# Second half of position 30's down weights as sixteen transfers of eight partitions

## The chip, the core and the metric

The kernel runs on one core of one Trainium2 chip. The metric is the device time of one execution in microseconds (us). Three runs of the kernel before took 1213.39 us (median), 1213.33 and 1214.49 us.

## The reference

One decoder layer over 256 tokens of width 1024, all in float32. The first part (a gated spatial MLP and a block attention, merged and normalised) ends near 270 us of the span and the change does not touch it. The second part is a routed feed-forward: each token goes to 4 of 32 experts, and for each expert

```
gu  = xe @ w_up[e] + b_up[e]          # w_up[e]: 1024 x 2048, 8 MB
g   = min(gu[:, :F], 7);  u = clip(gu[:, F:], -7, 7)
act = (u + 1) * (g * sigmoid(1.702 * g))
y   = act @ w_down[e] + b_down[e]     # w_down[e]: 1024 x 1024, 4 MB
```

The weighted sum of the experts' outputs is added to the residual and a last LayerNorm gives the result. Every expert's 12 MB of weights is read once, some 400 MB in all, for a few rows of tokens each.

## The kernel before

The 32 experts are sorted at run time into 32 positions; position 30 is the last but one. Each position has three steps: "a" and "b", the two halves of the up product, and "d", the down product. Each step's weights are two halves of 2 MB (128 partitions by 16 KB), named a0, a1, b0, b1, d0, d1. Positions 5 to 29 (`WHOLE`) load both halves of a step by one transfer of 4 MB; positions 30 and 31 load each half by its own.

The weights go into a ring of five buffers `R`, each of two half slots. `load_next(slot)` (line 176 and on) takes the next half in the list `order` and issues its transfer from the SyncE queue (SP), to the slot that was just released by the product that read it. So the order of transfers is that of the steps, and SP waits before a transfer for the product that frees the slot. Line 211 is the ordinary transfer. The last half of all (d1 of position 31) is cut by columns into four transfers of 512 KB, so that the last product can begin with the first quarter (line 209). The list ends:

```
... b0,b1 of 30   a0,a1 of 31   b0,b1 of 31   d0,d1 of 30   d0,d1 of 31
```

TensorE's order around these steps is written out: `step` calls `up_part` for a and b and `down_half` (line 729) for d, and between them small pieces that were put off by `later` (transposes of the activation, line 719; the spread of the routing weights, line 684; the scatter of a finished position, line 744). The down product of position 30 takes d0, then d1; then come the transposes for position 31 and the scatter of position 30, then d0 and the four quarters of d1 of position 31, and the last scatter. After that VectorE takes the statistics of the last LayerNorm (line 1124), a loop for left-over tokens is entered (line 1147), and four stores write the output.

Of the kernel before, what the change touches and what calls it, by code (L numbers as in the profile page):

```python
# [17 lines left out]
P = 128  # L18
# [6 lines left out]
NE = 32  # L25
# [2 lines left out]
WHOLE = range(5, 30)  # L28
LEFT_AT, RESIDUAL_AT, NORM_AT = 5, (7, 12), 17
W0, W1, W2, W3, W4, W5 = 9, 3, 9, 7, 5, 3  # L30
MS = {mybir.EngineType.PE}
STARTS = {mybir.EngineType.PE, mybir.EngineType.DVE, mybir.EngineType.Activation}

# [21 lines left out]
def tile_kernel(ctx: ExitStack, tc: tile.TileContext, x, ln_in_g, ln_in_b, w_in, gmlp_ln_g, gmlp_ln_b,  # L55
                w_spatial, b_spatial, w_branch_a, w_branch_b, w_out, ln_mix_g, ln_mix_b, w_router,
                b_router, w_up, b_up, w_down, b_down, ln_ffn_g, ln_ffn_b, out):
    nc = tc.nc
# [7 lines left out]
    def ps_mm():  # L66
        return bank["pool"].tile([P, 512], FT, name="mm", bufs=bank["mm"])
# [103 lines left out]
    def half(slot):  # L171
        return R[slot // 2][:, slot % 2 * 4096:slot % 2 * 4096 + 4096]
# [3 lines left out]
    def load_next(slot):  # L176
        done.append(slot)
        if len(ring) == len(order):
            return
        p, k = order[len(ring)]  # L180
        n = 2 if p in WHOLE else 1
        if len(done) < n:
            return
        slots = done[-n:]
        done.clear()
        for i, to in enumerate(slots):
            ring[p, k[0] + str(int(k[1]) + i)] = to
        if p not in expert_at:
            expert_at[p] = nc.values_load(dyn["ids"][0:1, p:p + 1], engines=[mybir.EngineType.SP], min_val=0,
                                          max_val=NE - 1)  # L190
        e, h = expert_at[p], int(k[1])
        if n == 2:
            assert h == 0 and slots[0] % 2 == 0 and slots[1] == slots[0] + 1
            to = R[slots[0] // 2]
        else:
            to = half(slot)
        if k[0] == "d":
            src = wd[e] if isinstance(e, int) else wd[bass.ds(e, 1)].rearrange("o p h n -> (o p) h n")
            if n == 2:
                to = to.rearrange("p (h n) -> p h n", h=2)  # L200
            else:
                src = src[:, h]
        else:
            src = wu[e] if isinstance(e, int) else wu[bass.ds(e, 1)].rearrange("o p n -> (o p) n")
            lo = 8192 * (k[0] == "b") + 4096 * h
            src = src[:, lo:lo + 4096 * n]
        if len(ring) == len(order):
            for j in range(4):
                nc.sync.dma_start(to[:, j * 1024:(j + 1) * 1024], src[:, j * 1024:(j + 1) * 1024])
        else:  # L210
            nc.sync.dma_start(to, src)

# [352 lines left out]
    for i in range(n_pieces):  # L565
# [29 lines left out]
        if nm == "A" and hf == 1:  # L595
            attend()
            for slot in (4, 5, 6, 7):
                load_next(slot)
        if nm == "B":
            to_T(G1, hTh, hTl, (hf,))  # L600
        if i >= n_pieces - 3:
            for slot in ((2, 3), (0,), (1,))[i - n_pieces + 3]:
                load_next(slot)
# [30 lines left out]
    sp2 = ctx.enter_context(tc.tile_pool(name="s2", bufs=1, reuse_waits="tile"))  # L634
    R.append(sp2.tile([P, 8192], FT, name="R4"))
    load_next(8)
    load_next(9)
    hT2 = sp2.tile([P, NC, 2 * GRP * CAP], FT, name="hT2")
# [438 lines left out]

    with tc.manual_schedule(engines=MS):
        def free(p, k):
            load_next(ring[p, k])  # L1080
# [66 lines left out]
    with tc.For_i(0, n_left) as i:  # L1147
# [27 lines left out]
        for j in range(2):  # L1175
            to = [ps_mm(), ps_mm()]
# [51 lines left out]
```

## Time and profile before

| | |
|---|---|
| median of three runs | 1213.39 us |
| the profiled execution's own time | 1214.27 us |
| its span, first to last instruction | 1212.6 us |
| mean granted TensorE clock | 0.964 |
| TensorE matmul busy | 1108.5 us (91%) |
| VectorE, ScalarE, GpSimd busy | 414.5, 214.9, 110.0 us |
| HBM read | 448.58 MB, 371 GB/s over the span |

The page gives the busy time of each engine, the span in 40 slices (from 333 us to 1182 us every slice has the DMA engines at 90% or more and 426 to 433 GB/s), the costliest groups of instructions with what ended the idle time before them, and the DMA transfers by line. The trace behind it answers for any stretch: an engine's instructions in order of time, who waited for whom, how long a transfer took from its issue to its landing (the moment its completion has fully arrived), and the mean busy share of the 16 DMA engines. Times are us from the span's start.

### The profile page before, as it was taken

What the parts mean: (1) busy time and instruction counts of PE and PEld (TensorE: products, weight loads), DVE (VectorE), ACT (ScalarE), POOL (GpSimd) and SP (SyncE); (2) the same over time, 40 slices, a digit from 0 to 9 for tenths busy, and PEclk for the clock granted to TensorE, in tenths of its full rate; (3) what the DMA queues carried; (4) which work ended last, traced back from release to release, by engine and by line L of the source; (5) the groups of instructions that cost most, each with busy time, mean ns of one, the idle gap of its engine ahead of it and who ended that gap; (6) DMA issues with size and microseconds to landing.
All of it is one profiled execution on the core that took longest, in us unless ns stands there. A gap on an engine that the chain in (4) does not pass through costs nothing. (4 is left out here: it accounts for less than half of the span.)

```text
span 1212.6 us, 21803 instructions
## 1 busy us (share of the span) xinstructions
PE 1108.5 (91%) x9725; PEld 578.8 (48%) x9725; DVE 414.5 (34%) x787; ACT 214.9 (18%) x355; POOL 110.0 (9%) x121
## 2 busy tenths in 40 slices
PE   8999999998989889889999998999999899999793
PEld 6777888874424343343444343434333434344231
DVE  7964645564323121313122231413222221221213
ACT  5445643422101000010000010101010100010010
POOL 2800200000000000001000000100100010100000
PEclk9999999999999989889999998999999998999888
DMA  9554557665899999999999999999999999999993
GB/s 355 188 208 147 222 186 303 252 255 236 337 429 433 430 430 430 431 431 431 430 432 430 430 433 430 431 429 430 430 433 432 431 430 430 431 431 430 426 428 135
DMA packets 44208, 451.06 MB, mean 372 GB/s; under 512 B 2968, under 2 KB 3628, under 8 KB 26064
## 3 DMA queue, kind: packets, MB, share of 16 engines
q1 hardware_dynamic: 43504, 449.47, 88.5%
q8 instruction: 78, 1.28, 0.4%
q10 hardware_dynamic: 608, 0.16, 0.1%
q14 instruction: 18, 0.15, 0.0%
HBM read 448.58 MB, written 1.05 MB: 371 GB/s over the span
## 5 line engine op out<-in xcount | busy, mean ns | idle before, releaser
L702 PE MATMUL mm<-R,hT 128*32 128x512 f32 x3136 | 378.4, 609 | 13.7 <-DMA R<-in_w_up_dram 13.7
L729 PE MATMUL at<-R,actT 128*32 128x256 f32 x3328 | 217.6, 402 | 17.6 <-DMA R<-in_w_down_dram 7.4
L702 PEld LDWEIGHTS mm<-R,hT 128*32 128x32 f32 x3136 | 89.8, 111 | 198.0 <-issue 173.9
L708 DVE TENSOR_SCALAR gg<-mm 64x512 f32<-64x512 f32 x49 | 33.5, 683 | 389.2 <-PE mm L702 389.2
L729 PEld LDWEIGHTS at<-R,actT 128*32 128x32 f32 x3328 | 100.7, 115 | 110.2 <-issue 29.9
L711 POOL TENSOR_TENSOR gg<-gg,sg 64x512 f32<-64x512 f32 x52 | 66.5, 1278 | 845.1 <-ACT sg L709 845.1
L479 DVE TENSOR_TENSOR wlo<-R,whi 128x1024 fp32r<-128x1024 f32 x80 | 112.4, 1416 | 76.1 <-ACT whi L471 75.7
L529 PE MATMUL mm<-whi,hTh 128*128 128x512 f32 x256 | 100.9, 402 | 0.8 <-ACT R L488 0.8
L529 PE MATMUL mm<-wlo,hTh 128*128 128x512 f32 x256 | 99.9, 398 | 0.5 <-DVE wlo L479 0.5
L529 PE MATMUL mm<-whi,hTl 128*128 128x512 f32 x256 | 99.9, 398 | 0.0
L471 ACT ACTIVATE whi<-R 128x1024 fp32r<-128x1024 f32 x80 | 84.3, 1056 | 86.7 <-PE mm L529 81.5
L709 ACT ACTIVATE sg<-gg 64x512 f32<-64x512 f32 x52 | 32.8, 631 | 284.9 <-DVE gg L708 261.4
L736 ACT ACTIVATE y<-at 128x256 f32<-128x256 f32 x52 | 20.0, 384 | 338.1 <-PE at L729 338.1
L661 PEld LDWEIGHTS tp<-pt,xn 128*128 128x128 f32 x464 | 58.6, 198 | 32.9 <-DVE hT L666 21.2
L661 PE MATMUL tp<-pt,xn 128*128 128x128 f32 (+2 forms) x464 | 69.0, 294 | 0.5 <-DVE pt L653 0.4
L744 PE MATMUL ac<-y,qt 32*128 32x256 f32 x832 | 60.6, 406 | 0.5 <-ACT y L736 0.5
L669 ACT ACTIVATE hT<-tp,lm 128x128 f32<-128x128 f32 (+2 forms) x58 | 25.8, 445 | 195.3 <-PE tp L661 195.3
L744 PEld LDWEIGHTS ac<-y,qt 32*128 32x128 f32 x832 | 38.1, 187 | 37.5 <-issue 35.2
L719 PEld LDWEIGHTS tp<-ident,act 64*128 64x128 f32 x208 | 28.8, 209 | 54.2 <-issue 17.2
L529 PEld LDWEIGHTS mm<-wlo,hTh 128*128 128x128 f32 x256 | 48.0, 188 | 12.9 <-DVE wlo L479 1.7
L721 DVE COPY actT<-tp 128x256 f32<-128x256 f32 x52 | 22.1, 425 | 93.7 <-PE tp L719 93.6
L529 PEld LDWEIGHTS mm<-whi,hTh 128*128 128x128 f32 x256 | 48.4, 190 | 11.8 <-ACT R L488 0.9
(265 smaller groups left out, 835.7 us busy)
## 6 DMA issues: line engine op xcount, KB each, us to landing
R<-in_w_up_dram SPq DMA_DIRECT2D x50, 4096.0 KB, 32.1
R<-in_w_down_dram SPq DMA_DIRECT2D x25, 4096.0 KB, 34.1
R<-in_w_up_dram SPq DMA_DIRECT2D x28, 2048.0 KB, 11.6
R<-in_w_in_dram SPq DMA_DIRECT2D x13, 2048.0 KB, 9.6
R<-in_w_down_dram SPq DMA_DIRECT2D x13, 2048.0 KB, 32.7
R<-in_w_branch_a_dram SPq DMA_DIRECT2D x2, 2048.0 KB
R<-in_w_branch_b_dram SPq DMA_DIRECT2D x2, 2048.0 KB, 9.0
R<-in_w_out_dram SPq DMA_DIRECT2D x2, 2048.0 KB
```

The source lines that it names most:

```text
L471: nc.scalar.activation(hi, w, AF.Copy)
L479: nc.vector.tensor_tensor(lo, w, hi.bitcast(FT), op=OP.subtract)
L529: nc.tensor.matmul(ps[t], (a_l if k == 1 else a_h)[:, c, t * P:(t + 1) * P], (lo if k == 2 else hi)[:, cc], start=c == 0 and k == 0, stop= ...
L661: nc.tensor.matmul(ps[:, i * w:(i + 1) * w], zn[:, t, c * P:(c + 1) * P], pt[:, t, :w], start=t == 0, stop=t == T - 1)
L669: nc.scalar.activation(dst[:, c, :w], ps[:, i * w:(i + 1) * w], AF.Identity, scale=lm[:, 0, c:c + 1], bias=lm[:, 1, c:c + 1])
L702: nc.tensor.matmul(ps[n * CAP:(n + 1) * CAP], xs[:, c], w[:, o:o + 512], start=False, stop=c == NC - 1)
L708: nc.vector.tensor_scalar(gg, ps[:2 * CAP], LIMIT, None, op0=OP.min)
L709: nc.scalar.activation(sg, gg, AF.Sigmoid, scale=SW_ALPHA)
L711: nc.gpsimd.tensor_tensor(gg, gg, sg, op=OP.mult)
L719: nc.tensor.transpose(ps[:, c * 2 * CAP:(c + 1) * 2 * CAP], v[:, c], ident[:2 * CAP, :2 * CAP])
L729: nc.tensor.matmul(py[n * CAP:(n + 1) * CAP, :256], at[:, c, h], w[:, o:o + 256], start=h == 0 and c == 0, stop=h == 1 and c == 3)
L744: nc.tensor.matmul(to[n // 2][:, n % 2, t * 256:(t + 1) * 256], qt[s, t], y[s], start=start and t == 0, stop=stop and t == T - 1)
```

## The change

`load_next` gets a third case. For d1 of position 30 the one transfer of 128 partitions by 16 KB becomes sixteen, each of eight partitions (128 KB). All other transfers, and every product, stay as they are.

```
+EIGHTHS = (NE - 2, "d1")
 ...
         if len(ring) == len(order):
             for j in range(4):
                 nc.sync.dma_start(to[:, j * 1024:(j + 1) * 1024], src[:, j * 1024:(j + 1) * 1024])
+        elif (p, k) == EIGHTHS:
+            for j in range(0, P, 8):
+                nc.sync.dma_start(to[j:j + 8], src[j:j + 8])
         else:
             nc.sync.dma_start(to, src)
```

## Rows read from the trace of the kernel before

**Rows 1.** Costliest groups: instruction, count | busy us, mean ns | idle before, releaser.
```profile
L729 PE MATMUL at<-R,actT 128*32 128x256 f32 x3328 | 217.6, 402 | 17.6 <-DMA R<-in_w_down_dram 7.4
```

**Rows 2.** Timeline of PE at the end: start us, us, instructions, [idle before <-releaser].
```profile
1180.63 1.93 PE L729 MATMUL at<-R,actT 128*32 128x256 f32 x32 [0.16 <-SPq L1147]
1185.50 1.93 PE L729 MATMUL at<-R,actT 128*32 128x256 f32 x32 [2.94 <-SPq L1147]
...
1188.94 1.15 PE L744 MATMUL ac<-y,qt 32*128 32x256 f32 x16
1190.37 2.37 PE L729 MATMUL at<-R,actT 128*32 128x256 f32 x40 [0.28 <-DMA R<-in_w_down_dram]
...
1195.40 0.64 PE L729 MATMUL at<-R,actT 128*32 128x256 f32 x8 [0.61 <-DMA R<-in_w_down_dram]
```

**Rows 3.** DMA issues at 1114.05, 1140.69, 1146.69, 1154.33: KB, us to landing.
```profile
R<-in_w_up_dram SPq DMA_DIRECT2D x1, 2048.0 KB, 37.4
R<-in_w_down_dram SPq DMA_DIRECT2D x1, 2048.0 KB, 39.9
R<-in_w_down_dram SPq DMA_DIRECT2D x1, 2048.0 KB, 38.8
R<-in_w_down_dram SPq DMA_DIRECT2D x1, 2048.0 KB, 36.0
```

**Rows 4.** Stretches: us, busy of PE, PEld, DVE, ACT, POOL, PEclk, DMA share, GB/s.
```profile
1182.60:1185.50 2.90, 0.00 (x0) 0.00 (x0) 0.68 (x1) 0.00 (x0) 0.68 (x1) 1.00 0.86 362
1185.50:1187.40 1.90, 1.90 (x33) 0.97 (x33) 0.00 (x0) 0.00 (x0) 0.00 (x0) 1.00 0.52 222
```

**Rows 5.** DMA in 1186 to 1198: packets in all, and queue 8's share.
```profile
DMA packets 341, 1.73 MB, mean 144 GB/s; under 512 B 41, under 2 KB 41, under 8 KB 300
...
q8 instruction: 1, 0.02, 0.6%
```

**Rows 6.** Timeline of SP, transfers as issued: start us, us, line, count.
```profile
1114.05 24.45 SPq L211 DMA_DIRECT2D R<-in_w_up_dram  x6
1140.69 0.33 SPq L211 DMA_DIRECT2D R<-in_w_down_dram  x1
1146.69 0.33 SPq L211 DMA_DIRECT2D R<-in_w_down_dram  x1
...
1156.39 0.33 SPq L209 DMA_DIRECT2D R<-in_w_down_dram  x1
...
1170.91 0.33 SPq L209 DMA_DIRECT2D R<-in_w_down_dram  x1
```

**Rows 7.** Waits of SP's queue, 1138 to 1172: us in total, times, longest.
```profile
SPq L209 <- DMA R<-in_w_up_dram: 14.1, 4, 4.3
```

**Rows 8.** DMA in 0 to 3.3: all packets, and ScalarE's queue (q10).
```profile
DMA packets 90, 0.31 MB, mean 93 GB/s; under 512 B 8, under 2 KB 16, under 8 KB 90
...
q10 hardware_dynamic: 16, 0.00, 0.5%
```

**Rows 9.** Issue cost on SP: line 209's duration in ns; five issues without a wait.
```profile
L209 SPq DMA_DIRECT2D R<-in_w_down_dram x4: 333/333/337, 1156.4 to 1170.9; - x4
...
17.12 0.40 SPq L219 DMA_DIRECT2D R<-in_gmlp_ln_g_dram  x1
...
19.48 0.60 SPq L223 DMA_DIRECT2D R<-in_b_up_dram  x1
```

**Rows 10.** Transfers into an empty queue (268 to 269.2, and the stores).
```profile
R<-in_w_up_dram SPq DMA_DIRECT2D x2, 2048.0 KB, 7.2
...
out_dram<-R SPq DMA_DIRECT2D x4, 256.0 KB, 2.0
```

**Rows 11.** An earlier wait: PE timeline, then two stretches as in rows 4.
```profile
1127.16 3.64 PE L702 MATMUL mm<-R,hT 128*32 128x512 f32 x16 [5.02 <-DMA R<-in_w_up_dram]
...
1125.90:1129.30 3.40, 2.14 (x12) 0.59 (x16) 0.00 (x0) 0.00 (x0) 0.00 (x0) 0.50 1.01 434
1129.30:1132.70 3.40, 3.40 (x24) 1.22 (x16) 0.00 (x0) 0.00 (x0) 0.00 (x0) 0.50 0.98 419
```

More of the change, by code (lines that the diff above doesn't have):

```diff
@@ L30 @@
 W0, W1, W2, W3, W4, W5 = 9, 3, 9, 7, 5, 3
+EIGHTHS = (NE - 2, "d1")
 MS = {mybir.EngineType.PE}
@@ L209, in load_next @@
                 nc.sync.dma_start(to[:, j * 1024:(j + 1) * 1024], src[:, j * 1024:(j + 1) * 1024])
+        elif (p, k) == EIGHTHS:
+            for j in range(0, P, 8):
+                nc.sync.dma_start(to[j:j + 8], src[j:j + 8])
         else:
```

## Prediction, made before the changed kernel ran

> **What bounds the kernel now.** I read the page's busy times and 40 slices first (TensorE 91% busy, DMA engines full from 333 us on), then the costliest groups, then the last 30 us by timeline. A busy TensorE does not settle what bounds the end: the down product's idle time is ended by weights [rows 1], and at the end every product of a down half starts when its weights land. Adding the time to landing to the issue times, d0 of position 30 lands at 1140.69 + 39.9 = 1180.59, d1 at 1146.69 + 38.8 = 1185.49, d0 of position 31 at 1154.33 + 36.0 = 1190.33 [rows 3]; the products start at 1180.63, 1185.50 and, with the first quarter, 1190.37, and the last quarter's at 1195.40 [rows 2]. So the last landing sets the end: 1195.4, then 0.64 us of matmuls to 1196.04 and an unchanged tail of 16.6 us to 1212.6.
>
> Two more things are to be seen there. First, the 16 DMA engines do not run level. After 1186 only 1.73 MB are moved [rows 5], yet d0 and d1 of position 31 (4.19 MB) have still to land: 60% of them is already there. The engines' busy share falls from 0.86 before 1185.5 to 0.52 behind it [rows 4]: about eight engines are done by some 1187, the other eight work until 1195.4 (1.73 MB at half of 430 GB/s is 8.0 us). The early eight lead by some 8.4 us, and a transfer lands with its last engine. Second, SP holds transfers back. Its four quarters, issued from 1156.39 to 1170.91 [rows 6], each waited for the landing of an up half, 14.1 us in four waits [rows 7]. The up half of 1114.05 lands at 1151.45 and d0 of position 30, six transfers later, at 1180.59 [rows 3], so landings are 4.86 us apart: 1156.3 (b1 of position 30), 1161.2, 1166.0, 1170.9 (b0 of position 31), 1175.7, 1180.6. The first quarter goes out at the first of these moments, the last at the fourth. Counted in order of issue that is each time the eighth transfer before it: at most eight are under way.
>
> **The change part by part.** *Issue.* One transfer goes, sixteen come, at the same place in the order; the same rule gives the first eighth the landing of position 29's down weights (it goes at 1146.7 as before), the second 1151.5, then 1156.3, 1161.2, 1166.0, 1170.9, 1175.7, and the eighth of them waits for d0 of position 30: about 1180.7, where the whole d1 before was issued at 1146.69. Behind it stand eight more eighths, d0 of position 31 and the four quarters, thirteen issues that went out by 1170.91 before. They find their counters free as the earlier eighths land, so SP's pace is what they cost: at least 0.33 us each, and (19.48 - 17.12) / 4 = 0.59 us where five went out with no wait [rows 9]. I take 0.55, nearer to the second, since line 209 also works out an address between two issues: d0 of position 31 goes at 1180.7 + 9 x 0.55 = 1185.7, 31 us later than before.
>
> *Transfer.* A load of eight rows is in the trace once at the start: 16 packets by ScalarE's queue, eight of them under 512 B [rows 8]: eight rows of 512 B and eight small completion writes, where sixteen engines would need sixteen. So I take an eighth to run on eight engines, one row of 16 KB each, at 4.86 / 8 = 0.61 us. [...] On those engines nine eighths are left at 1180.7. The stores land 2.0 us behind their issue [rows 10], 0.6 of it their 256 KB at 430 GB/s, so the delay is 1.4: 1180.7 + 1.4 + 9 x 0.61 = 1187.6 for the last eighth, 4.86 for d0, 1190.33 to 1195.40 = 5.07 for the quarters: 1197.5. On the other eight, which have nothing from 1180.6 on, d0 is a transfer into an empty queue, 7.2 us [rows 10]: 1185.7 + 7.2 + 5.07 = 1198.0. The two groups end level, and that has a price: a code fetch (0.6% of 16 engines over 12 us, 1.15 us on one engine [rows 5]) now delays the end wherever it falls, where before it could fall on an early engine. Between 0 and 1.15 I take 0.5: last landing 1198.4, 3.0 us later than 1195.4. Bounds: with 0.33 us an issue, 1.0 us of delay and no fetch 1197.1 (+1.7); with 0.59 and a whole fetch 1199.5 (+4.1). Were an eighth spread over all sixteen engines, the line of d0 into an empty queue would stand: the same number.
>
> *TensorE.* d0's product ends at 1182.56; d1's starts at 1187.6 in place of 1185.5, an idle time of 5.0 in place of 2.94 us. There is one such wait in the trace: 5.02 us before 1127.16, and the granted clock is 0.50 (1.2 GHz of 2.4) from 1125.9 to 1132.7; sixteen matmuls took 3.64 us behind it [rows 11]. So I expect d1's product at 3.86 us instead of 1.93, to 1191.5. From its end to the end of the scatter it was 2.66 us (1187.43 to 1190.09 [rows 2]); with part of it at half clock 3.4, to 1194.9; then 64 matmuls, 3.86 us: 1198.8. The last landing and its 0.64 us give 1199.0: the half clock is just covered. Without that cover (the clock down to the end) it would be 3 to 4 us more. The extra waits of the product on sixteen landings instead of one lie before 1187.6 but for the last and cost nothing.
>
> *Sum.* The end moves by +3.0 us: 1217.3 on the profiled execution's own 1214.27, which stands 0.9 us above the runs' median; on the median 1213.39 + 3.0 = 1216.4.
>
> **The rivals.**
> *The eighths fall on late engines* (all of them, or a mix of early and late). Then those never run dry: from 1180.6 they have sixteen rows of 0.61 = 9.8 us, to 1190.4, then 4.86 and 5.07: 1200.3, +4.9 us, 1218.3. Nothing in the rows tells the early eight from the others; for it stands that any late engine among the eight is enough, against it that early eight and all sixteen both give the forecast.
> *The eighths even out the engines* (faster). If the wait on the eighth transfer before does not bind, all sixteen are issued in time, 2 MB move from the late eight to the early eight: the early end at 1187 + 4.9 = 1191.9, the late at 1195.4 - 4.9 = 1190.5, 3.5 us sooner: 1209.9. It decides where the early engines run out of the first seven eighths: 1180.6 - 8.4 + 7 x 0.61 = 1176.5. If the eighth eighth is issued before, this happens; I have it at 1180.7. For it: the lead of 8.4 us is real, and 4.9 is nearly its half. Against it: four waits out of four in [rows 7].
> *Each eighth pays its whole way.* If transfers of one row per engine do not overlap, nine take 2.0 us each [rows 10], 18 in place of 6.9: +14 us, 1227. Against it: the quarters land 1.27 us apart. [...]
> *It is hidden.* If SP issues faster and the first packets come sooner than I have them, what is left is under 2.4 us.
>
> **How the numbers follow.** Forecast 0.62, of which 0.13 lies under 0.2% (2.4 us, about what a measurement of this kernel can tell from no change); late engines 0.20; evened out 0.08; whole way 0.04; hidden 0.06. Slower: 0.49 + 0.20 + 0.04 = 0.73; same: 0.13 + 0.06 = 0.19; faster 0.08. The range runs from the forecast's lower part (+1.0, 1214.4) to beyond the late engines (+6.0, 1219.4); it leaves out the faster case, the whole way and a little at both edges.
>
> **What would show it.** SP's line of the eighths with seven waits for landings 4.86 us apart, the eighth issue near 1180.7 and d0 of position 31 near 1185.7; a DMA share well under 0.9 between 1176 and 1187, where it was over 0.86 until 1185.5; d1's product starting near 1187.6 (1190.4 for late engines, 1182.6 for the faster rival) with the clock at 0.50 behind it; the last quarter's product near 1198.4. If the eighth eighth goes out before 1177, the prediction is wrong at its first step; if it does and the end is still not sooner, at the transfer.

## The result, and the profile after

The changed kernel takes 1232.66 us (median of 4 runs, 1230.67 to 1236.01), the kernel before 1213.94 beside it (4 runs, 1213.33 to 1215.93): a ratio of 1.0157, 95% interval 1.014 to 1.0175. The direction was forecast, the size was not: +18.7 us in place of +3.0, 13 us above the range. The profiled execution's own time is 1232.76 us, its span 1231.0, the mean granted clock 0.951; against the 1212.6 of before the span grew by 18.4 us, and these are what the rows below divide.

The down product's group, line 729 before and 733 now (columns as in [rows 1]): nearly the same busy time, the idle time ahead of it 12.7 us longer.

```profile
L733 PE MATMUL at<-R,actT 128*32 128x256 f32 x3328 | 221.9, 409 | 30.3 <-SPq L1151 16.0
```

The timeline of PE at the end of the changed kernel, which answers to [rows 2]: d0 of position 30, then d1, then d0 and the quarters of position 31 in one piece.

```profile
1184.60 1.93 PE L733 MATMUL at<-R,actT 128*32 128x256 f32 x32 [1.37 <-DMA R<-in_w_down_dram]
1202.56 3.64 PE L733 MATMUL at<-R,actT 128*32 128x256 f32 x32 [16.03 <-SPq L1151]
...
1210.04 4.44 PE L733 MATMUL at<-R,actT 128*32 128x256 f32 x64
```

Three differences make the whole loss. d0 of 30 starts 4.0 us later than before (1184.60 against 1180.63). From there to d1 it is 17.96 us in place of 4.87: +13.1. From d1's start to the end of the last product it is 11.92 us (1214.48 - 1202.56) in place of 10.54: +1.4. The sum, 18.5, is the span's growth within a tenth; the tail behind the last product is 16.5 us, as before.

SP's transfers of the same stretch, which answer to [rows 6], and SP's waits from 1184 to 1195 (columns as in [rows 7]):

```profile
1146.07 47.51 SPq L213 DMA_DIRECT2D R<-in_w_down_dram  x16
1194.58 0.36 SPq L215 DMA_DIRECT2D R<-in_w_down_dram  x1
1195.66 3.82 SPq L210 DMA_DIRECT2D R<-in_w_down_dram  x4
```

```profile
SPq L213 <- DMA R<-in_w_down_dram: 10.5, 9, 5.4
```

The sixteen eighths take SP 47.5 us to issue, and d0 of position 31 goes at 1194.58 (forecast 1185.7). Of the nine waits the longest, 5.4 us, is the eighth issue's for d0 of 30. The other eight, 5.1 us together, are for the eighth transfer before, which is now itself an eighth: the first ones had not all landed. The trace also keeps the steps of a transfer's semaphore, sixteen for an ordinary transfer on the 16 DMA engines; a step is read here as one engine's report that its share has landed. For the first eighth there are eight reports, six from 1171.0 to 1175.5 and two at 1184.1 and 1185.2; in the second to the seventh, too, the last two come 8 to 12 us behind the sixth. So, read this way, an eighth runs on eight engines, and two of these eight lag. The last report of the sixteenth eighth comes at 1202.1, just before d1's product.

Stretches of the changed kernel, columns as in [rows 4]:

```profile
1166.00:1170.00 4.00, 2.88 (x3) 0.99 (x4) 0.00 (x0) 0.97 (x2) 0.00 (x0) 0.50 1.00 422
1170.00:1174.00 4.00, 4.00 (x12) 0.90 (x14) 0.00 (x0) 0.60 (x1) 0.00 (x0) 0.50 0.98 213
1174.00:1178.00 4.00, 4.00 (x28) 1.02 (x24) 0.00 (x0) 0.00 (x0) 0.00 (x0) 0.56 0.63 195
...
1198.00:1202.00 4.00, 0.00 (x0) 0.00 (x0) 0.00 (x0) 0.00 (x0) 0.00 (x0) 0.50 1.00 328
1202.00:1206.00 4.00, 3.44 (x32) 1.62 (x32) 0.00 (x0) 0.00 (x0) 0.00 (x0) 0.50 0.97 396
```

The second row is the surprise: 0.98 of the engines' time is busy, and they move 213 GB/s, half of the row above. An engine's share says how long its packets took, not how much they carried. In the last two rows the granted clock is 0.50, the lower of the two levels that the trace shows (0.50 and 1.00), in the wait before d1's product and under it. What a packet took is worked out from the transfers of one stretch (packets in all, those under 512 B, which are taken for the completion writes, 32 of them after against 32 reports in the same 6 us, and the queue's share of 16 engines). From 1170 to 1176, before:

```profile
DMA packets 180, 2.61 MB, mean 434 GB/s; under 512 B 21, under 2 KB 21, under 8 KB 21
...
q1 hardware_dynamic: 180, 2.61, 101.7%
```

and after:

```profile
DMA packets 105, 1.20 MB, mean 199 GB/s; under 512 B 32, under 2 KB 32, under 8 KB 32
...
q1 hardware_dynamic: 105, 1.20, 88.2%
```

Before, 1.017 x 16 x 6 = 97.6 us for 180 - 21 = 159 packets of 16 KB: 0.61 us each. After, 84.7 us for 73: 1.16 us each. In this stretch the rows took nearly twice as long, and not those of the eighths alone: d0 of position 30, an ordinary transfer issued at 1139.02, landed 4 us late.

### The profile page after: what moved, and what is told of

Read it like the earlier page. It is cut to its first block, busy times and chain, and to the rows that moved or that the text cites. A ratio compares the mean times of both kernels' runs of the same rounds, so it can differ in the third digit from the quotient of the medians.

```text
span 1231.0 us, 21852 instructions
## 1 busy us (share of the span) xinstructions
PE 1114.4 (91%) x9725; PEld 581.2 (47%) x9725; DVE 412.9 (34%) x787; ACT 215.0 (17%) x355; POOL 111.4 (9%) x121
## 3 DMA queue, kind: packets, MB, share of 16 engines
q8 instruction: 78, 1.28, 0.4%
HBM read 448.58 MB, written 1.05 MB: 365 GB/s over the span
## 5 line engine op out<-in xcount | busy, mean ns | idle before, releaser
L733 PE MATMUL at<-R,actT 128*32 128x256 f32 x3328 | 221.9, 409 | 30.3 <-SPq L1151 16.0
L483 DVE TENSOR_TENSOR wlo<-R,whi 128x1024 fp32r<-128x1024 f32 x80 | 112.8, 1420 | 76.5 <-ACT whi L475 76.2
L533 PEld LDWEIGHTS mm<-wlo,hTh 128*128 128x128 f32 x256 | 48.0, 188 | 11.8 <-DVE wlo L483 0.6
```

Of the source, the lines that this page charges most:

```text
L483: nc.vector.tensor_tensor(lo, w, hi.bitcast(FT), op=OP.subtract)
L533: nc.tensor.matmul(ps[t], (a_l if k == 1 else a_h)[:, c, t * P:(t + 1) * P], (lo if k == 2 else hi)[:, cc], start=c == 0 and k == 0, stop= ...
L733: nc.tensor.matmul(py[n * CAP:(n + 1) * CAP, :256], at[:, c, h], w[:, o:o + 256], start=h == 0 and c == 0, stop=h == 1 and c == 3)
```

## The experiments

Times are medians, the ratio is against the kernel before on the same chip. There are two runs of the kernels with the SBUF or HBM alone spread and with every second partition, and four to ten of the others. In the first diff the lines of the changed kernel stand with a minus; most of the later ones show only the new lines. "Gap" is the time from d0's product of position 30 to d1's (before 4.87, after 17.96), "packet" the mean time of a 16 KB packet from 1170 to 1176, worked out as above (before 0.61, after 1.16). This mean takes in ordinary rows as well as those of the eighths, and it scatters: the two kernels of "TensorE's clock" below, with 60 and 76 filler matmuls, have the change's transfers, and in the same 6 us they give 1.02 and 0.86 us (86.3 and 73.0 us for 85 packets each).

```profile
DMA packets 121, 1.39 MB, mean 232 GB/s; under 512 B 36, under 2 KB 36, under 8 KB 36
...
q1 hardware_dynamic: 121, 1.39, 89.9%
```

```profile
DMA packets 125, 1.40 MB, mean 233 GB/s; under 512 B 39, under 2 KB 39, under 8 KB 39
...
q1 hardware_dynamic: 124, 1.39, 76.0%
```

So 0.61 can be told from 0.86 and more, and values from 0.86 to 1.28 are not ranked here.

**Which rows an eighth takes.** Three kernels, each with sixteen transfers of eight partitions, one row to an engine. The first takes every fourth partition of 32:

```
-            for j in range(0, P, 8):
-                nc.sync.dma_start(to[j:j + 8], src[j:j + 8])
+            for b in range(0, P, 32):
+                for r in range(4):
+                    nc.sync.dma_start(to[b + r:b + 32:4], src[b + r:b + 32:4])
```

> Sixteen transfers of eight partitions as in the change, but each takes every fourth partition of a group of 32 (rows b+r, b+r+4, ... b+r+28), on the SBUF side and on the HBM side, so that the same rows land in the same partitions. Size, count, order and waits are those of the change. Theory A (eight neighbouring partitions share a way into SBUF and the eight engines get in each other's way there): a 16 KB packet takes 0.61 us again, and what is left is the wait for the eighth transfer before and the two late engines among the eight: 1180.6 + 16 x 0.61 + 4.86 + 5.07 = 1200.3 for the last landing, 1218.5 us in all (1217 to 1221). Theory B (the eight rows of one transfer are 128 KB in one piece of HBM and the engines collide there): the same, 1218.5. Theory C (a transfer with one packet per engine costs each engine a fixed part, whatever the addresses): packets stay near 1.1 us or gaps stay between them, 1232.

The second spreads the rows in the SBUF alone, the third in HBM alone; of the same two loops only the last line differs. In both, this half's rows land in other partitions than in the changed kernel, so its product is of permuted rows.

```
+                    nc.sync.dma_start(to[b + r:b + 32:4], src[b + 8 * r:b + 8 * r + 8])
```

> As the strided one, but the source stays eight neighbouring rows of HBM, so rows of this one weight half land in other partitions (part of the computation is changed: the half's rows are permuted). Theory A (collision in SBUF): 1218.5. Theory B (collision in HBM): 1232. Theory C (fixed part per transfer): 1232.

```
+                    nc.sync.dma_start(to[b + 8 * r:b + 8 * r + 8], src[b + r:b + 32:4])
```

> The other way round: eight neighbouring partitions of SBUF, filled from every fourth row of HBM (the half's rows are permuted, so part of the computation is changed). Theory A: 1232. Theory B: 1218.5. Theory C: 1232.

Measured: both 1223.00 (ratio 1.0082, 1.0066 to 1.0099), SBUF alone 1221.74 (1.0066, 1.0046 to 1.0086), HBM alone 1232.24 (1.0152, 1.0123 to 1.0182). Where the rows lie in the SBUF is half the loss; where they lie in HBM is none of it. The first two are some 2 us and 1 us above the 1217 to 1221 that were expected of a collision in the SBUF. Packets with both spread, 1170 to 1176:

```profile
DMA packets 129, 1.58 MB, mean 264 GB/s; under 512 B 32, under 2 KB 32, under 8 KB 32
...
q1 hardware_dynamic: 128, 1.57, 62.6%
```

60.1 us for 96 packets, 0.63 us each; by the same working 0.61 with the SBUF alone spread (62.0 us for 101) and 0.97 with HBM alone (76.5 for 79):

```profile
DMA packets 141, 1.66 MB, mean 277 GB/s; under 512 B 39, under 2 KB 39, under 8 KB 39
...
q1 hardware_dynamic: 140, 1.65, 64.6%
```

```profile
DMA packets 112, 1.29 MB, mean 216 GB/s; under 512 B 33, under 2 KB 33, under 8 KB 33
...
q1 hardware_dynamic: 112, 1.29, 79.7%
```

The products with both spread, d0 and d1 of position 30:

```profile
1180.41 1.91 PE L734 MATMUL at<-R,actT 128*32 128x256 f32 x32
1192.07 3.64 PE L734 MATMUL at<-R,actT 128*32 128x256 f32 x32 [9.75 <-SPq L1152]
```

d0 is on time again, and the gap is 11.7 us. The 0.63 holds for the stretch shown: from 1188 to 1191, with d0 of position 31 under way beside the last eighths, the same kernel has 46.4 us for 50 packets, 0.93 us each.

**Every second partition.** Two ranges of sixteen, `to[b + r:b + 16:2]`.

> Eighths of every second partition of a group of 16, on both sides. Where eight neighbours make a packet of 1.1 us and every fourth of 32 one of 0.61, the way into SBUF is shared by some group of neighbours. If by groups of two: as every fourth, 0.61 us and 1223. [...] If by groups of eight or more: near 1.1 us, 1232.

1231.12 us (1.0138, 1.0113 to 1.0164), packet 0.95. In time this is hardly better than neighbours (1232.66): near the 1232 that was expected of groups of eight or more, and 8 us above the 1223 of groups of two.

**Eight transfers of sixteen partitions.** With eight transfers in place of sixteen no issue of this half waits for another of its own, so the rows' collision stands alone. Neighbouring rows first, then every eighth partition:

```
+            for j in range(0, P, 16):
+                nc.sync.dma_start(to[j:j + 16], src[j:j + 16])
```

> Eight transfers of sixteen neighbouring partitions: the wait for the eighth transfer before holds no issue of the half, so the collision in the SBUF stands alone. If engines that write neighbouring partitions slow each other to the 1.05 to 1.3 us a row seen after the change, the half takes 8.4 to 10.4 us on each engine in place of 4.9, and the late engines have no slack: +3.5 to +5.5 us, 1217 to 1219.5. If the loss needed the queue to be held up as well, 1214.

```
+            for j in range(8):
+                nc.sync.dma_start(to[j::8], src[j::8])
```

> As the run before, but each transfer takes every eighth partition on both sides, so the rows written at one time lie eight partitions apart. Neighbours as the cause: 1214, as before the change. Cutting a half by partitions as such as the cause (a row to an engine, whatever the rows): the same +3.5 to +5.5 us as the run before.

Neighbours 1226.04 (1.0096, 1.0081 to 1.0111), spread 1222.78 (1.0074, 1.006 to 1.0087). Both are misses: the first lost more than forecast, because d0 of 30 is late as well (1185.37) on top of a gap of 10.74, with a packet of 1.11; the second was to lose nothing if only neighbours collide. Its packets from 1170 to 1176:

```profile
DMA packets 113, 1.25 MB, mean 208 GB/s; under 512 B 37, under 2 KB 37, under 8 KB 37
...
q1 hardware_dynamic: 113, 1.25, 101.0%
```

97.0 us for 76 packets, 1.28 us each, with rows eight partitions apart. "Neighbours" was too simple.

**Every eighth partition of 64, and the upper half first.** Rows eight partitions apart were slow in transfers of sixteen rows (1.28 us), rows four apart were not in transfers of eight (0.63). The first kernel here takes the distance of eight to transfers of eight rows. The second asks whether the ordinary transfers' rows, under way beside the first eighths, play a part: then it can matter which half comes first. The second diff is against the first kernel of this section, every fourth partition of 32.

```
+            for b in range(0, P, 64):
+                for r in range(8):
+                    nc.sync.dma_start(to[b + r:b + 64:8], src[b + r:b + 64:8])
```

> Sixteen transfers of eight partitions, each of every eighth partition of 64, on both sides. With every fourth partition of 32 the packets took 0.61 us each, eight apart over 128 they took 1.2. [...] If only rows closer than four partitions slow each other, they take 0.61 and the whole 1223, as with every fourth.

```
-            for b in range(0, P, 32):
+            for b in (64, 96, 0, 32):
                 for r in range(4):
```

> Every fourth partition of 32, as in the first such run, but partitions 64 to 127 before 0 to 63. [...] If only the rows of one eighth slow each other, nothing changes: 1223.

Every eighth: 1232.05 us (1.0155, 1.0141 to 1.0169), the full loss of the change, where 1223 was expected if only rows closer than four partitions slow each other. Upper half first: 1227.39 (1.0119, 1.0102 to 1.0135), +14.2 us on its runs of before, where the lower half first had +9.5; 1223 was expected if only the rows of one eighth slow each other. Packets of the two, 1170 to 1176:

```profile
DMA packets 116, 1.29 MB, mean 216 GB/s; under 512 B 37, under 2 KB 37, under 8 KB 37
...
q1 hardware_dynamic: 116, 1.29, 86.1%
```

```profile
DMA packets 86, 0.97 MB, mean 162 GB/s; under 512 B 26, under 2 KB 26, under 8 KB 26
...
q1 hardware_dynamic: 85, 0.97, 72.6%
```

1.05 us (82.7 us for 79) and 1.18 (69.7 for 59). The products of position 30 with the upper half first:

```profile
1184.35 3.64 PE L734 MATMUL at<-R,actT 128*32 128x256 f32 x32 [4.57 <-DMA R<-in_w_down_dram]
1196.14 3.36 PE L734 MATMUL at<-R,actT 128*32 128x256 f32 x32 [8.15 <-DMA R<-in_w_down_dram]
```

d0 is 3.9 us later than with the lower half first (1184.35 against 1180.41), the gap is nearly the same, 11.8 us. The rows of an eighth are the same in both orders, yet the packets are slow (1.18) with the upper half first, and d0 is late: what they meet there must be the ordinary rows, which is argued from the order alone. With the lower half first, packets of rows four partitions apart within 32 took 0.61 and 0.63 us, those of neighbours 1.16, of rows two apart 0.95, of rows eight apart 1.05 and 1.28. Which rows collide, and by what they do, is not shown beyond these distances. In time neighbours and rows two apart are about the same, 1232.7 and 1231.1 us.

**The wait and the issues without the collision.** The half cut by columns, first into sixteen, then into eight.

```
+            for j in range(16):
+                nc.sync.dma_start(to[:, j * 256:(j + 1) * 256], src[:, j * 256:(j + 1) * 256])
```

> The same half as sixteen transfers of 128 KB, but cut by columns: all 128 partitions by 1 KB, so all sixteen engines take part in each. The count of transfers and so the waits of SP are those of the change, nothing goes on eight engines. If the wait for the eighth transfer before is a cost of its own: the eighth piece goes out at 1180.7, d0 of position 31 near 1185.7, and the end is later by 2.5 to 3.5 us: 1216 to 1217.5. If the waits cost nothing and all of the loss is the slow transfers: 1213 to 1214.5. If any transfer of 128 KB is slow: 1225 or more.

```
+            for j in range(8):
+                nc.sync.dma_start(to[:, j * 512:(j + 1) * 512], src[:, j * 512:(j + 1) * 512])
```

> The half as eight column pieces (128 partitions by 2 KB, 256 KB each). The eighth piece still waits for d0 of position 30 (1180.6), but only one more issue stands between it and d0 of position 31, which goes out near 1181.3 in place of 1186 with sixteen pieces. If the wait by itself costs: 1216 to 1221, as with sixteen. If it is the issues that queue behind the wait, nine at 0.57 us, while the engines run dry: the late engines still hold 4.3 us of pieces at 1180.6 and never run dry, 1213 to 1214.5, the same as before.

Sixteen: 1220.99 us (1.0058, 1.0038 to 1.0079), outside all that was expected of it. Eight: 1214.22 (1.0001, 0.999 to 1.0012), as expected if the wait by itself costs nothing. SP's transfers with sixteen, then with eight:

```profile
1147.62 38.60 SPq L213 DMA_DIRECT2D R<-in_w_down_dram  x16
1186.47 0.33 SPq L215 DMA_DIRECT2D R<-in_w_down_dram  x1
```

```profile
1145.74 34.93 SPq L213 DMA_DIRECT2D R<-in_w_down_dram  x8
1180.95 0.33 SPq L215 DMA_DIRECT2D R<-in_w_down_dram  x1
```

With sixteen, d0 of position 31 goes at 1186.47, as forecast for the change (1185.7). With eight it still goes 27 us later than before and costs nothing: the wait is covered. With sixteen, d0 goes 5.5 us later still, for the eight issues more, and the last quarter's product starts 5.6 us later than before:

```profile
1201.00 0.64 PE L733 MATMUL at<-R,actT 128*32 128x256 f32 x8 [0.62 <-DMA R<-in_w_down_dram]
```

Sixteen pieces also leave less work ahead of the wait: the engines' busy share from 1174 to 1178 is 0.57, with eight pieces 0.99. The two were not separated. So the moment of d0's issue was forecast rightly, but its price was not: +7.5 us (1220.99 - 1213.49) where the forecast had +3.0 for everything.

**TensorE's clock.** The change with filler matmuls between d0's and d1's product, 60 and then 76:

```
+                    if p == NE - 2 and h == 0:
+                        warm(60, ps_mm())
```

> The changed kernel with 60 matmuls on constants put on TensorE between the two halves of position 30's down product, into a PSUM buffer that nobody reads, so that TensorE works while it waits for the eighths. The transfers are untouched. In the changed kernel the product of d1 starts at 1202.56 at the half clock (3.64 us for 32 matmuls), and TensorE ends 2.7 us behind the last landing of 1211.8. If the clock is what costs these: d1's product takes 1.93, all between it and d0 of position 31 is done by 1207.2, the end is the last landing's plus 0.64, 2.0 us sooner than in the changed kernel: 1230.5. If the clock costs nothing: 1232.5 or, as the filler delays, more.

> The change with 76 filler matmuls in place of 60 between the two halves of position 30's down product, 16.6 us at full clock, so that they reach to the landing of d1. If the half clock behind the wait is what keeps the end 2.7 us behind the last landing, the end comes 0.7 to 1 us behind it and the whole gains 1.5 to 2 us on the change: 1230.5 to 1231. If the transfers set the end whatever the clock, the same as the change, 1232.5, or more where the filler runs past the landing.

60: 1234.25 us (1.0161, 1.0137 to 1.0185), no gain. 76: 1230.76 (1.0139, 1.0123 to 1.0155). The end of PE with 60 (filler, d1, the last product), then with 76 (the same, and the last quarters):

```profile
1189.08 13.12 PE L264 MATMUL mm<-ones 128*128 128x512 bf16 x60
1204.65 2.69 PE L733 MATMUL at<-R,actT 128*32 128x256 f32 x32 [2.45 <-SPq L1153]
...
1211.17 4.29 PE L733 MATMUL at<-R,actT 128*32 128x256 f32 x64
```

```profile
1185.81 16.98 PE L264 MATMUL mm<-ones 128*128 128x512 bf16 x76
1202.72 1.93 PE L733 MATMUL at<-R,actT 128*32 128x256 f32 x32
...
1207.24 2.80 PE L733 MATMUL at<-R,actT 128*32 128x256 f32 x48
1210.51 0.64 PE L733 MATMUL at<-R,actT 128*32 128x256 f32 x8 [0.47 <-DMA R<-in_w_down_dram]
1211.77 0.64 PE L733 MATMUL at<-R,actT 128*32 128x256 f32 x8 [0.62 <-DMA R<-in_w_down_dram]
```

The filler of 60 ended 2.45 us too soon, and the products behind that wait ran slow again (2.69 us for 32 matmuls, 4.29 for 64). With 76 the granted clock is 1.00 from 1202.6 on, and the products take the times of the kernel before (1.93 for 32) and wait for the last quarters, as in [rows 2]. From d1's start to the end of the last product it is 9.7 us (1212.41 - 1202.72) in place of the change's 11.92: some 2 us of its loss are the half clock behind the long wait, which the medians agree with (1230.76 and 1232.66).

**The eighths in the middle.** `EIGHTHS = (4, "d1")`: the same cut 26 positions earlier.

> The change moved to d1 of position 4, some 850 us before the end, where the DMA engines are just full and TensorE has work behind them. If a hole in the transfers is lost for good because the DMA engines bound all that follows: 8 to 16 us more than before, 1221 to 1230. If the buffers ahead absorb it: 1213 to 1215. The two late engines cannot matter there (all engines run level until 350 us).

1226.51 us (1.0134, 1.0074 to 1.0193; 1221.8 to 1238.6). Two stretches of this kernel, then of the kernel before:

```profile
398.00:406.00 8.00, 7.04 (x60) 2.50 (x56) 2.38 (x5) 0.63 (x1) 1.28 (x1) 1.00 0.76 238
406.00:414.00 8.00, 4.79 (x58) 1.66 (x50) 1.24 (x4) 0.00 (x0) 0.00 (x0) 1.00 0.70 228
```

```profile
398.00:406.00 8.00, 7.04 (x64) 2.41 (x60) 2.26 (x4) 0.63 (x1) 1.28 (x1) 1.00 0.99 426
406.00:414.00 8.00, 8.00 (x89) 3.04 (x85) 1.36 (x4) 0.00 (x0) 0.00 (x0) 1.00 1.06 455
```

(188 + 227) GB/s over 8 us are 3.3 MB that were not moved, 7.7 us at 430 GB/s, and the span of this run is 7.5 us longer (1220.1): 770 us of further loading give nothing back. In this kernel, which its transfers bound from there to the end, the hole was lost although it lay so early. The trace is of the fastest of the four runs (1221.8); the others were slower by 1.4, 8.0 and 16.8 us, and what they lost besides is not known.

## Why the prediction was wrong

*The failed step: "So I take an eighth to run on eight engines, one row of 16 KB each, at 4.86 / 8 = 0.61 us."* Eight engines is right (eight reports for each eighth), and 0.61 is right for the rows of the kernel before. It was carried over from transfers of 128 rows, on sixteen engines, to one of eight neighbouring rows, whose price no row of the kernel before shows: 1.16 us in the stretch from 1170. From the eighth issue to the landing of d1 the sum had 1.4 + 9 x 0.61 = 6.9 us, and d1's product started 17.96 us after d0's. That spreading the rows in the SBUF brings 0.61 back in that stretch, and spreading them in HBM does not (0.97), was shown; every kernel with rows at distance 1, 2 or 8 has packets of 0.86 us or more there.

*"Early eight and all sixteen both give the forecast."* Wrong as the case here: the eighths' engines include two late ones, the condition of the first rival (a mix). Each eighth lands with these two, and so the ninth to the sixteenth issue wait, 5.1 us in eight waits. That rival's sum, sixteen rows behind d0, is the right form. With the rows spread on both sides it nearly holds as it stands: d1's product starts at 1192.07, where the rival has 1190.4. In the change 16 rows in 17.96 us are 1.12 each, where it had 0.61. With this 1.12, which is taken from the gap itself, and d0 4.0 us later, its 1200.3 becomes 1184.6 + 17.9 + 4.86 + 5.07 = 1212.4; with the longer filler, where TensorE waits for it, the last quarter's product starts at 1211.77.

*"The eighth of them waits for d0 of position 30: about 1180.7."* The wait is there, d0 was not in time: it landed 4 us later. That its rows met those of the first eighths is argued from the two orders of halves, of which one delays d0 and the other doesn't. No step of the forecast let the added transfers slow the ones already under way; the eighth issue, which hangs on that landing, went with it.

*The wait on the eighth transfer before, and SP's pace.* Right for as long as ordinary transfers stood ahead: six waits for up halves, 29.5 us in all, 4.9 each, and with columns d0 of 31 goes at 1186.47. For the change itself the pace was set by landings, not by 0.55 us an issue, and d0 went 8.9 us later than forecast: 4.0 from d0 of 30, the rest from those waits.

*"The half clock is just covered."* It was not: the wait grew to 16 us, and cost some 2 us. The traces give the clock as a share of full speed; the 2.4 GHz of the forecast fit, as an estimate, the kernel before, where at a share of 1.00 nine matmuls of 512 columns took 2.10 us (line 260 at 268.86, 0.38 us for one of them): 0.215 us for each further one, 2.4 columns a ns.

*"Each eighth pays its whole way"* (1227) came nearest in time, by the wrong mechanism: a fixed price for each transfer would fall on spread rows too, and they take 0.63 us from 1170 to 1176. *"The eighths even out the engines"* needed the eighth issue before 1177; it waits for d0 of 30, which landed near 1184.6.

So of 18.7 us some 7.5 go with the wait and the issues (sixteen columns) and some 11.1 with the collision (sixteen neighbours in eight transfers, 1226.04 - 1214.98), the clock being a part of either. That the two add up so nearly is a reading of separate kernels; within one kernel the parts were not separated.

**Open.** That two of the eighths' eight engines lag is seen, but not which two or why. Nor was it resolved why every second partition is nearly as slow as neighbours, or which of the rows under way at one time slow each other. No version beat the kernel before: eight columns equal it.

## What to carry to other kernels

Before a load is cut by partitions, ask which rows will be written at the same moment: a per-row price read from full 128-partition transfers (0.61 us) held here for rows four partitions apart within 32, lower half first, and not for neighbours (1.16) or rows eight apart (1.05 and 1.28), and a DMA share near 1 at half the GB/s (0.98 at 213) was the sign that it didn't. Try a cut by columns instead, and into no more pieces than the transfers that may be under way (eight here: the issues that waited for a landing waited for the eighth transfer before): the same half in eight column pieces cost nothing, in sixteen 7.5 us; no number between was tried. Where an added transfer runs beside others, price what it does to them as well as its own time.

## What the runs showed of the chip that was not expected

From 1170 to 1176 rows of 16 KB took 0.61 to 0.63 us where the eighths' rows lay four partitions apart within 32, lower half first, and 0.86 to 1.28 us at distances of one, two and eight; with the upper half first distance four had 1.18. At the end of the load the engines were not level: of the eight that carry an eighth, as the eight reports are read, two landed the first seven 8 to 12 us behind the other six. One issue of every fourth partition kept SP for 0.64 us, one of a block of eight neighbours in the SBUF for 0.28. And the engines' busy share was 0.98 at 213 GB/s, where it was 1.00 at 422 just before, so it cannot be read as bandwidth.
